# Both MLP products of a decoder layer as seven products of halves, with the activations kept in DRAM between them

## The chip, the cores and the metric

The kernel runs on one core of a Trainium2 chip. The metric is the device time of one execution in microseconds, given as the median of several runs. The engines are named as the profile names them: PE is the matrix engine (TensorE), PEld its weight loads, DVE the vector engine, ACT the scalar engine, POOL GpSimd, and SP the engine whose queue issues most DMAs. ACT issues some DMAs too.

## The reference

One decoder layer on x of 1024 positions by 1024 features, all in float32: three parallel token mixers, merged by gates, then an MLP.

```python
h = rms_norm(x, norm_mix[layer])
proj = h @ w_in[layer]
...
branches = jnp.stack([oa, ob, oc], axis=0)
y = jnp.einsum('nbsm,nmd->bsnd', branches, w_branch[layer])
gate = jax.nn.sigmoid(mg.reshape(B, S, N_BRANCH, D_MODEL).astype(jnp.float32)).astype(y.dtype)
x = x + jnp.sum(gate * y, axis=2) @ w_out[layer]
h = rms_norm(x, norm_mlp[layer])
x = x + jnp.square(jax.nn.relu(h @ w_up[layer])) @ w_down[layer]
```

oa, ob and oc are the outputs of the mixers (differential, sliding-window and block-sparse attention). The change concerns what follows y: the product with w_out (called wo), the normalization, and the two products of the MLP, w_up (wu, 1024 x 4096) and w_down (wd, 4096 x 1024).

## The kernel before

**Products.** Every float32 matrix product is done in three matmuls. `split` (L87) writes a value as a high part, a copy on ACT (L90), and a low part, a subtraction on DVE or POOL (L91), each of a type that PE takes at full rate. `mm3` (L112) then adds high·high, high·low and low·high into one bank of PSUM. A bank holds 128x512 numbers; one matmul here multiplies 128x128 by 128x512. `weight` (L93) loads 128x512 weights from DRAM into a raw tile (`wr`) on SP's queue and splits them into `wh` and `wl`, low part on POOL.

**Order.** The order of PE's instructions is that of the code. The order of the instructions of DVE, ACT, POOL and of SP's queue is chosen by a scheduler when the program is built, from what is ready in its own model. Each engine then executes its list strictly in order. Tiles come from pools; with `bufs=n` a name has n buffers in turn, and an instruction that writes one waits for the last reader of what was there. A pool that is released gives its memory to the pools that are opened after it, with the same kind of wait.

**The end of the program** is `merge_and_mlp` (L1151). The branches are multiplied by their matrices and gated; g tiles (from a DRAM tile `gd`, L1122) hold the gates, and `mh`, `ml` receive the two parts of the merged result for all 1024 positions, with the features on the partitions (eight tiles k of 128).

*The wo stage.* The eight tiles of wo are loaded through two raw buffers (`xn`, L1203) and split, with the low part on DVE and POOL by turns. x is loaded into the eight tiles `x1` (L1208, ACT's queue). For each tile t of 128 positions and each half of 512 features PE does 24 matmuls (8 k by 3), and DVE adds the bank to x1 (L1216). `norm_transpose` (L125) squares x1 on ACT (L130), scales it on DVE (L132), and gives back the transposes (L139), which PE does one tile later; the transposed, normalized tile is split into `mh` and `ml`, which wo no longer needs there.

*Up and down.* `up_block` forms two of the 32 groups of 128 hidden features at a time: 24 matmuls for each group and each half of the positions, then Relu on ACT (L1245), the square on DVE (L1246) and a split into `uh`, `ul`. `down_block` multiplies these two groups by their part of wd for all eight tiles and both halves, 6 matmuls a bank, and DVE adds each bank to x1 (L1262). PE does one up block ahead of the down block that uses the one before. The last down block also sends each tile of x1 to `out`.

In all the MLP has 1536 matmuls of 128x512 for up and 1536 for down, and 16 small transposes between.

## Time and profile before

| | |
|---|---|
| median of 3 runs | 2139.64 us (2138.3 to 2140.58) |
| the profiled execution's own time | 2133.3 us |
| its span, first to last instruction | 2131.5 us |
| mean granted PE clock | 0.990 |
| busy DVE / ACT / POOL | 58% / 41% / 32% of the span |
| wo stage begins, first matmul of up, last of down | about 1322, 1418.65, 2127.26 us |

In the profile's rows a group of instructions is named by line, engine, operation and output<-input with buffer numbers left out. A timeline row gives start and duration; in brackets stands how long the engine had been idle before and what ended the idle time. Matmuls overlap in the pipeline, so their durations add to more than the time that passes: what one costs is the distance from its start to the next start. Busy shares are averages over the whole program; the stage that the change touches is the last third of the span.

### The profile page before, as it was taken

How to read it: one execution, taken by the hardware profiler on the slowest of the kernel's cores; microseconds unless marked ns; L12 is line 12 of the kernel's file. 1: busy time of each engine (PE TensorE's matmuls, PEld its weight loads, DVE VectorE, ACT ScalarE, POOL GpSimd, SP SyncE). 2: the span in 40 equal slices, each digit the busy share in tenths (PEclk: the TensorE clock that was granted, in tenths of full speed). 3: DMA queues.
4: the chain of work that ended last, by engine and by line, in shares of the span. 5: the costliest groups of instructions: out<-in, count | busy, mean ns of one | idle time of the engine just before them, and what ended most of it. 6: DMA issues, size and time to landing. Idle time of an engine off the chain costs nothing.

```text
span 2131.5 us, 29645 instructions
## 1 busy us (share of the span) xinstructions
PE 2025.8 (95%) x10190; PEld 1680.4 (79%) x10190; DVE 1228.5 (58%) x3027; ACT 878.3 (41%) x2358; POOL 676.9 (32%) x965
## 2 busy tenths in 40 slices
PE   6999999988899999999998898999999999999999
PEld 6777777788688878888877776888888888888887
DVE  5757677788757676567777537333334433344334
ACT  5355555566546555455555433122222122211210
POOL 4455345454361121261313065022222122211210
PEclk9999999999999999999999898999999999999999
DMA  6131012011301111221324275211111111111101
GB/s 209 49 100 50 3 53 56 21 42 37 97 26 59 49 58 52 69 65 54 118 90 161 86 255 188 79 48 61 50 46 49 40 55 55 45 45 40 54 7 79
DMA packets 85027, 149.14 MB, mean 70 GB/s; under 512 B 10052, under 2 KB 31044, under 8 KB 84876
## 3 DMA queue, kind: packets, MB, share of 16 engines
q1 hardware_dynamic: 80204, 133.61, 20.0%
q10 hardware_dynamic: 4672, 13.63, 1.8%
q8 instruction: 80, 1.31, 0.3%
q14 instruction: 71, 0.58, 0.1%
HBM read 119.89 MB, written 31.26 MB: 71 GB/s over the span
## 4 chain that ended last, share of the span: by engine, by line
PE 77%; DVE 8%; ACT 5%; DMA 3%; issue 3%; POOL 2%; SPq 0%; DVEq 0%; ACTq 0%; POOLq 0%
PE mm L115 19%; PE mm L116 18%; PE mm L117 18%; PE sc L697 5%; PE tr L745 3%; PE sc L115 2%; PE sc L116 2%; PE sc L117 2%; ACT p L729 2%; PE ac L887 2%; PE ac L888 2%; DMA g<-gd 1%; PE tr L544 1%; DVE sc L721 1%; POOL wl L91 1%
## 5 line engine op out<-in xcount | busy, mean ns | idle before, releaser
L91 POOL TENSOR_TENSOR wl<-wr,wh 128x512 fp32r<-128x512 f32 (+3 forms) x278 | 348.1, 1261 | 698.2 <-ACT wh L90 645.6
L90 ACT ACTIVATE wh<-wr 128x512 fp32r<-128x512 f32 (+3 forms) x290 | 170.8, 596 | 420.7 <-PE mm L117 239.0
L1262 DVE TENSOR_TENSOR x<-x,mm 128x512 f32<-128x512 f32 x256 | 174.7, 687 | 141.0 <-PE mm L117 141.0
L697 PE MATMUL sc<-st 128*128 128x256 f32 (+5 forms) x736 | 200.5, 354 | 16.1 <-ACT p L729 15.8
L1246 DVE TENSOR_TENSOR u<-v 128x512 f32<-128x512 f32 x64 | 64.9, 1014 | 241.0 <-ACT v L1245 241.0
L115 PE MATMUL mm<-mh,wh 128*128 128x512 f32 x512 | 202.0, 395 | 0.2 <-ACT mh L90 0.2
L116 PE MATMUL mm<-ml,wh 128*128 128x512 f32 x512 | 201.9, 394 | 0.2 <-DVE ml L91 0.2
L117 PE MATMUL mm<-mh,wl 128*128 128x512 f32 x512 | 201.8, 394 | 0.0
L116 PE MATMUL mm<-wl,uh 128*128 128x512 f32 x512 | 199.3, 389 | 0.0
L115 PE MATMUL mm<-wh,uh 128*128 128x512 f32 x512 | 199.3, 389 | 0.0
L117 PE MATMUL mm<-wh,ul 128*128 128x512 f32 x512 | 199.2, 389 | 0.0
L90 ACT ACTIVATE ph<-tr 128x384 fp32r<-128x384 f32 (+3 forms) x280 | 138.3, 496 | 117.8 <-PE tr L745 99.9
L91 DVE TENSOR_TENSOR pl<-tr,ph 128x384 fp32r<-128x384 f32 (+3 forms) x280 | 155.5, 558 | 44.4 <-ACT ph L90 40.9
L697 PEld LDWEIGHTS sc<-st 128*128 128x128 f32 x736 | 125.6, 190 | 56.2 <-ACT p L729 24.0
L115 PE MATMUL mm<-hh,wh 128*128 128x512 f32 x384 | 159.5, 415 | 0.0
L117 PE MATMUL mm<-hh,wl 128*128 128x512 f32 x384 | 152.0, 396 | 0.0
L116 PE MATMUL mm<-hl,wh 128*128 128x512 f32 x384 | 151.9, 396 | 0.0
L745 PE MATMUL tr<-ident,p 128*128 128x128 f32 x792 | 132.1, 280 | 15.4 <-ACT o L875 7.9
L742 POOL MEMSET ph<- 128x128 f32 x152 | 34.5, 227 | 298.9 <-PE ac L887 245.5
L729 ACT ACTIVATE p<-sc,mc 128x256 f32<-128x256 f32 (+5 forms) x200 | 106.7, 538 | 50.2 <-DVE mc L721 48.0
L887 PE MATMUL ac<-ph,st 128*128 128x256 f32 x392 | 110.6, 300 | 17.7 <-DVE ob L894 11.3
L115 PE MATMUL mm<-wh,hh 128*128 128x384 f32 (+1 forms) x320 | 125.0, 391 | 0.0
(253 smaller groups left out, 4741.9 us busy)
## 6 DMA issues: line engine op xcount, KB each, us to landing
wr<-wu SPq DMA_DIRECT2D x64, 256.0 KB, 2.6
wr<-wd SPq DMA_DIRECT2D x64, 256.0 KB, 2.9
gd<-go SPq DMA_DIRECT2D x48, 256.0 KB, 2.0
g<-gd SPq DMA_DIRECT2D x48, 256.0 KB, 3.0
wr<-wg SPq DMA_DIRECT2D x40, 256.0 KB, 2.7
wr<-wbr SPq DMA_DIRECT2D x40, 256.0 KB, 3.0
x<-x ACTq DMA_DIRECT2D x16, 512.0 KB, 6.2
wr<-wa SPq DMA_DIRECT2D x32, 192.0 KB, 3.1
```

What stands on the lines that cost most here:

```text
L90: nc.scalar.activation(hi, src, AF.Copy)
L91: (eng or nc.vector).tensor_tensor(lo, src, hi.bitcast(F32), op=ALU.subtract)
L115: mm(out, lh, rh, start=first, stop=False)
L116: mm(out, lh, rl, start=False, stop=False)
L117: mm(out, ll, rh, start=False, stop=last)
L697: self.nc.tensor.matmul(ps[:, off:off + k1 - k0], q[:, t * P:(t + 1) * P], k[:, k0:k1], start=i == 0, stop=i == 1)
L729: self.nc.scalar.activation(p, ps, AF.Exp, bias=m, scale=-1.0, accum_out=l)
L745: nc.tensor.transpose(pt[0:rows, o:o + P], src, self.ident)
L887: nc.tensor.matmul(ac, v, ph, start=first, stop=False)
L888: nc.tensor.matmul(ac, v, pl, start=False, stop=last)
L1246: nc.vector.tensor_tensor(u, v, v, op=ALU.mult)
L1262: nc.vector.tensor_tensor(x1[t][:, cs], x1[t][:, cs], ps, op=ALU.add)
```

## The change

The program after the merge is a new function, `tail`. A matrix product of two matrices cut into 2x2 blocks is formed of seven block products instead of eight, with sums of blocks as operands:

- Of the left matrix the sums s1 = 21 + 22, s2 = s1 − 11, s3 = 11 − 21, s4 = 12 − s2 are formed, of the right one t1 = 12 − 11, t2 = 22 − t1, t3 = 22 − 12, t4 = 21 − t2 (numbers name blocks by row and column). Product i uses the operands of the tables `ASIDE` and `BSIDE`.
- Product 2 accumulates on the bank of 1, 7 on that of 6, and 3 on that of 5.

*Up.* The hidden features are the rows and the positions the columns of the result; the 32 groups are taken as 16 pairs (p, p + 16). A pair has 7 products of 4 k by 3 matmuls: 84 for one pair, 1344 in all. The weight sums s1 to s4 of a pair are formed on DVE and split with the low part on POOL. The sums t1 to t4 of the activations (positions 0 to 511 against 512 to 1023) are made once in the wo stage, by `operands`, for t = 4 to 7, which needs `rb`, copies of the transposes of tile t − 4; so the tiles are taken in the order 0, 4, 1, 5, 2, 6, 3, 7. Two x1 buffers are used, and x1 goes to DRAM (`xd`). In `up_pair` DVE puts the result together out of the banks, ACT does Relu and the square, DVE forms the four sums that down needs as its left operand, and seven tiles of 128x512 go to DRAM (`ud`) for each pair.

*Down.* It begins when up has ended. x1 comes back from `xd` on ACT's queue (8 loads), into memory that up's operands held. Two pairs make a block: for each of the seven products two tiles u come from `ud` and are split on DVE, and two wd operands are split on POOL, which also forms the sums t1 to t4 of wd; 4 banks get 6 matmuls each, 168 in a block, 1344 in all. DVE adds each bank to x1, or, for products 1, 6 and 7, to sums `a1`, `a6`, `a7`. After the last block's products 6 and 7 DVE adds these sums to x1, in 20 more operations.

The core of the diff:

```diff
+    ORDER = (1, 6, 5, 2, 7, 4, 3)
+    ASIDE = {1: "11", 2: "12", 3: "s4", 4: "22", 5: "s1", 6: "s2", 7: "s3"}
+    BSIDE = {1: "11", 2: "21", 3: "22", 4: "t4", 5: "t1", 6: "t2", 7: "t3"}
...
+        xp = tc.alloc_tile_pool(name="xp", side="left", **kw)
...
         for k in range(KT):
-            raw = up.tile([P, D], F32, name="xn", tag="xn", bufs=2)
+            raw = xp.tile([P, D], F32, name="xn", tag="xn", bufs=2)
             nc.sync.dma_start(raw, a["wo"][k])
             self.split(*wo[k], raw, nc.vector if k % 2 else nc.gpsimd)
...
+                if t < 4:
+                    for half in range(2):
+                        r = xp.tile([P, 512], F32, name="rb", tag=f"rb{half}", bufs=1)
+                        self.first[half] = r
+                        nc.scalar.activation(r, ps[half], AF.Copy)
+                        ks = slice(half * 4, half * 4 + 4)
+                        self.split(mh[:, ks, ts], ml[:, ks, ts], wide(r), nc.gpsimd)
+                    return
+                b11, b21 = self.first
+                tmp = lambda: xp.tile([P, 512], F32, name="tt", tag="tt", bufs=3)
+                t1, t2 = tmp(), tmp()
+                nc.vector.tensor_tensor(t1, ps[0], b11, op=ALU.subtract)
+                nc.vector.tensor_tensor(t2, ps[1], t1, op=ALU.subtract)
+                self.split(mh[:, 4:8, ts], ml[:, 4:8, ts], wide(ps[1]))
+                self.split(th["t2"][0][:, :, js], th["t2"][1][:, :, js], wide(t2))
+                self.split(mh[:, 0:4, ts], ml[:, 0:4, ts], wide(t1), nc.gpsimd)
...
+        for t in (0, 4, 1, 5, 2, 6, 3, 7):
...
+            nc.sync.dma_start(xd[t], x1)
...
+            def product(i, chain=None):
+                w = splitted(get(self.ASIDE[i]), nc.gpsimd)
+                bh, bl, k0, s = moving[self.BSIDE[i]]
+                ps = o.ps[i] = o.ps[chain] if chain else self.mm()
+                for k in range(4):
+                    ks = slice(k * P, k * P + P)
+                    self.mm3(ps, w[0][:, ks], w[1][:, ks], bh[:, k0 + k, s], bl[:, k0 + k, s],
+                             k == 0 and not chain, k == 3, bool(chain))
...
+            def act(c):
+                u = temp()
+                nc.scalar.activation(u, c, AF.Relu)
+                nc.scalar.activation(u, u, AF.Square)
+                return u
...
+                for i in self.ORDER:
+                    nc.sync.dma_start(ud[p, i], get(self.ASIDE[i]))
...
+        tf.release()
         mp.release()
+        acc = tc.alloc_tile_pool(name="acc", side="left", **kw)
+        x1 = [acc.tile([P, D], F32, name=f"x1{t}") for t in range(NT)]
+        for t in range(NT):
+            nc.scalar.dma_start(x1[t], xd[t])
...
+        G = 2
+        order = (1, 6, 2, 7, 5, 4, 3)
...
+                for q in range(G):
+                    u = temp()
+                    nc.sync.dma_start(u, ud[b + q, i])
+                    forms.append((splitted(u, nc.vector), splitted(gets[q](self.BSIDE[i]), nc.gpsimd)))
...
+                    if i in sums and b == 0:
+                        nc.scalar.activation(dst, ps, AF.Copy)
+                    else:
+                        nc.vector.tensor_tensor(dst, dst, ps, op=ALU.add)
```

How the change moves instructions is seen in the lists of the two programs. **SP's queue at the end of the third branch, before.** g are the gates of that branch, wr<-wbr its weights, wr<-wu the first weights of up, and xn<-wo the raw tiles of wo:

```order
L1122 DMA g_14891<-gd_86 128x512
L1203 DMA xn_15428<-wo 128x1024
L1203 DMA xn_15432<-wo 128x1024
L1122 DMA g_14914<-gd_86 128x512
L100 DMA wr_15205<-wbr 128x512
L1122 DMA g_14931<-gd_86 128x512
L100 DMA wr_15230<-wbr 128x512
L1203 DMA xn_15436<-wo 128x1024
L1203 DMA xn_15440<-wo 128x1024
L100 DMA wr_15255<-wbr 128x512
```

The same queue with the change, from the load of g_15211, the tenth of the third branch's sixteen:

```order
L1122 DMA g_15211<-gd_86 128x512
L1245 DMA xn_15424<-wo 128x1024
L1245 DMA xn_15428<-wo 128x1024
L1122 DMA g_15236<-gd_86 128x512
L1122 DMA g_15261<-gd_86 128x512
L1245 DMA xn_15432<-wo 128x1024
L1245 DMA xn_15436<-wo 128x1024
L1122 DMA g_15286<-gd_86 128x512
L1122 DMA g_15311<-gd_86 128x512
L1245 DMA xn_15440<-wo 128x1024
L1245 DMA xn_15444<-wo 128x1024
```

Before, the first wo tiles are loaded among the gates of the second branch and the beginning of the third, and the last pair behind g_15286; with the change all eight come behind g_15211, and the last two (not shown) behind four loads of wu. Each pair waits for the low parts of the pair before.

**ACT at the end of up.** u are the last pair's activations, x10 to x17 the tiles of x1 that come back from xd:

```order
L1388 ACTIVATE u_18803<-u_18803 128x512
L1433 DMA x10_18848<-xd_15385 128x1024
L1433 DMA x11_18849<-xd_15385 128x1024
L1387 ACTIVATE u_18825<-u_18720 128x512
L1433 DMA x12_18850<-xd_15385 128x1024
L1433 DMA x13_18851<-xd_15385 128x1024
L1388 ACTIVATE u_18825<-u_18825 128x512
L1433 DMA x14_18852<-xd_15385 128x1024
```

And SP's queue at the same place, from the stores of the last pair's sums to the first loads of down:

```order
L1396 DMA ud_15386<-u_18829 128x512
L1396 DMA ud_15386<-u_18831 128x512
L1396 DMA ud_15386<-u_18836 128x512
L1457 DMA u_18876<-ud_15386 128x512
L1396 DMA ud_15386<-u_18840 128x512
L1457 DMA u_18888<-ud_15386 128x512
L1457 DMA u_18932<-ud_15386 128x512
```

Nothing of the kind stands in the program before, where x1 stays in place and u too. The loads of x1 wait for the last matmul of up, and u_18876 stands behind stores that wait for the last pair's sums; the loads and these stores use DMA semaphores in turn, and u_18876 also waits for the load of x13, u_18888 for that of x15.

**POOL in a block of down.** fl are low parts (of wr or of a sum u), u the sums t1 to t4, wr raw weights of wd:

```order
L91 TENSOR_TENSOR fl_19945<-u_19942,fh_19944 128x512
L91 TENSOR_TENSOR fl_19987<-wr_19706,fh_19986 128x512
L1224 TENSOR_TENSOR u_20114<-wr_20108,u_20112 128x512
L91 TENSOR_TENSOR fl_19997<-wr_19724,fh_19996 128x512
L1224 TENSOR_TENSOR u_20210<-wr_20090,wr_20092 128x512
L91 TENSOR_TENSOR fl_20037<-wr_20034,fh_20036 128x512
```

The load of wr_20108 goes into a buffer that fl_19987 reads last, and the sum that needs it is the next operation of POOL. Before, POOL did only the low parts of the weights in the MLP.

More of the change, by code (lines that the diff above doesn't have):

```diff
@@ L110, in spare, with mm3 @@
         return self.nc.vector if self.alone and k % 2 else self.nc.gpsimd
[L112 removed]
+    def mm3(self, out, lh, ll, rh, rl, first, last, more=False):
         mm = self.nc.tensor.matmul
[L115 to L117 removed]
+        mm(out, lh, rh, start=first, stop=False, skip_group_check=more)
+        mm(out, lh, rl, start=False, stop=False, skip_group_check=more)
+        mm(out, ll, rh, start=False, stop=last, skip_group_check=more)
     def rnorm(self, out, ss, n, width):
@@ L1194, in merge_and_mlp, with sums, get @@
                                                    op0=ALU.mult, op1=ALU.subtract)
+        self.wp.release()
+        self.tail(mp, mh, ml, halves)
+    ORDER = (1, 6, 5, 2, 7, 4, 3)
+    ASIDE = {1: "11", 2: "12", 3: "s4", 4: "22", 5: "s1", 6: "s2", 7: "s3"}
+    BSIDE = {1: "11", 2: "21", 3: "22", 4: "t4", 5: "t1", 6: "t2", 7: "t3"}
+    def sums(self, raw, new, side, eng):
+        made = {}
+        sub, add = ALU.subtract, ALU.add
+        rules = dict(s1=("21", "22", add), s2=("s1", "11", sub), s3=("11", "21", sub), s4=("12", "s2", sub),
+                     t1=("12", "11", sub), t2=("22", "t1", sub), t3=("22", "12", sub), t4=("21", "t2", sub))
+        def get(name):
+            if name not in made:
+                if name in rules:
+                    x, y, op = rules[name]
+                    x, y = get(x), get(y)
+                    made[name] = new()
+                    eng.tensor_tensor(made[name], x, y, op=op)
+                else:
+                    made[name] = raw(name)
+            return made[name]
+        return get
@@ new lines, in tail @@
+    def tail(self, mp, mh, ml, halves):
+        tc, nc, a = self.tc, self.nc, self.a
+        kw = dict(bufs=1, reuse_waits="tile")
+        H = FF // P // 2
+        xd = self.dram.tile([NT, P, D], F32, name="xd")
+        ud = self.dram.tile([H, 8, P, 512], F32, name="ud")
+        pre = tc.alloc_tile_pool(name="pre", side="right", **kw)
+        tf = tc.alloc_tile_pool(name="tf", side="left", **kw)
+        th = {n: [tf.tile([P, 4, 512], F32R, name=f"{n}{x}") for x in range(2)] for n in ("t2", "t3", "t4")}
@@ L1209, in merge_and_mlp @@
+        self.first = [None, None]
         late = []
-        for t in range(NT):
+        for t in (0, 4, 1, 5, 2, 6, 3, 7):
             ts = slice(t * P, t * P + P)
+            x1 = xp.tile([P, D], F32, name="x1", tag="x1", bufs=2)
+            nc.scalar.dma_start(x1, a["x"][ts, :])
             for s in halves:
@@ new lines, in tail, with form, raw @@
+        main = more = None
+        count = dict(f=0, r=0)
+        def form():
+            count["f"] += 1
+            if count["f"] <= 2:
+                return [pre.tile([P, 512], F32R, name=f"f{x}", tag=f"f{x}", bufs=2) for x in "hl"]
+            return [main.tile([P, 512], F32R, name=f"f{x}", tag=f"f{x}", bufs=10) for x in "hl"]
+        def raw(src):
+            count["r"] += 1
+            pool = pre if main is None or count["r"] % 2 else main
+            r = pool.tile([P, 512], F32, name="wr", tag="wr", bufs=4)
+            nc.sync.dma_start(r, src)
+            return r
@@ new lines, in up @@
+        def up(o, todo):
+            for i in todo:
+                o.product(i, {2: 1, 7: 6, 3: 5}.get(i))
+                o.after(i)
+        pairs = [up_pair(0)]
+        pairs[0].product(1)
+        for wp in reversed(wps):
+            wp.release()
+        main = tc.alloc_tile_pool(name="main", side="right", **kw)
+        pairs[0].after(1)
+        pairs.append(up_pair(1))
+        up(pairs[1], (1,))
+        pairs[0].product(2, 1)
+        while late:
+            late.pop()()
+        pairs[1].product(2, 1)
@@ new lines, in tail @@
+        xp.release()
+        more = tc.alloc_tile_pool(name="more", side="right", **kw)
+        for o in pairs:
+            o.after(2)
+        for o in pairs:
+            up(o, [i for i in self.ORDER if i not in (1, 2)])
+        for p in range(2, H):
+            up(up_pair(p), self.ORDER)
+        tf.release()
+        mp.release()
+        acc = tc.alloc_tile_pool(name="acc", side="left", **kw)
+        x1 = [acc.tile([P, D], F32, name=f"x1{t}") for t in range(NT)]
+        for t in range(NT):
+            nc.scalar.dma_start(x1[t], xd[t])
@@ L1280, in layouts @@
+        acc.release()
+        more.release()
+        main.release()
+        pre.release()
 def layouts(inputs):
```

179 lines of the change are left out of this document (115 added, 64 removed).

## The prediction

> **What bounds the kernel now.** I read the page's busy shares first, then its chain of waits, then busy time in windows over the stage that the change rewrites.
>
> ```profile
> PE 2025.8 (95%) x10190; PEld 1680.4 (79%) x10190; DVE 1228.5 (58%) x3027; ACT 878.3 (41%) x2358; POOL 676.9 (32%) x965
> ...
> PE 77%; DVE 8%; ACT 5%; DMA 3%; issue 3%; POOL 2%; SPq 0%; DVEq 0%; ACTq 0%; POOLq 0%
> ```
>
> TensorE is busy 95% of the span and holds 77% of the chain that ended last. An average could hide stages with another limit, so I look at the end of the program by itself. The columns of the windows are the stretch, its length, then busy time (and instructions) of PE, PEld, DVE, ACT and POOL, the granted clock, the DMA share and GB/s.
>
> ```profile
> 1320.00:1360.00 40.00, 35.65 (x147) 28.31 (x146) 20.68 (x27) 9.42 (x16) 4.95 (x4) 0.87 0.43 156
> ...
> 1420.00:1500.00 80.00, 79.52 (x347) 64.21 (x346) 31.37 (x40) 25.57 (x46) 30.25 (x23) 1.00 0.24 77
> 1500.00:1600.00 100.00, 100.00 (x435) 81.30 (x434) 39.29 (x53) 23.13 (x38) 23.39 (x19) 1.00 0.16 48
> ...
> 2000.00:2100.00 100.00, 100.00 (x437) 81.60 (x436) 39.99 (x58) 16.05 (x26) 12.72 (x10) 1.00 0.05 14
> ```
>
> From 1420 us on PE has no idle time at full clock, while DVE is busy 40%, ACT 23% and POOL 23%. The MLP is purely PE-bound: a matmul taken out is worth its full spacing, as long as no other engine becomes the limit. The spacing is read from the first and last matmul of the MLP on the timeline (start, duration, engine, line, operation).
>
> ```profile
> 1418.65 0.48 PE L115 MATMUL mm<-mh,wh 128*128 128x512 f32 x1
> ...
> 2127.26 0.39 PE L117 MATMUL mm<-wh,ul 128*128 128x512 f32 x1
> 2127.69 0.69 DVE L1262 TENSOR_TENSOR x<-x,mm 128x512 f32<-128x512 f32 x1 [0.67 <-PE mm L117]
> ```
>
> Between them the code issues 3072 matmuls of 128x512, so one costs (2127.26 − 1418.65)/3071 = 0.2307 us. The 0.39 us beside each row is its time in the pipeline, not its price. The two halves differ a little; a stretch of up shows 39 spacings in 9.10 us, 0.2333, which leaves 2 × 0.2307 − 0.2333 = 0.228 for down:
>
> ```profile
> 1426.91 0.39 PE L115 MATMUL mm<-mh,wh 128*128 128x512 f32 x1
> ...
> 1436.01 0.40 PE L115 MATMUL mm<-mh,wh 128*128 128x512 f32 x1
> ```
>
> **The sum, part by part.** All of it is made against the profiled execution, 2133.3 us; the median shown, 2139.64 us, lies 6.3 us above it, and I carry the difference to the median.
>
> **Removed.** Seven products for eight leave 2 × 1344 = 2688 matmuls. 384 × 0.2307 = **−88.6 us**.
>
> **wo stage.** The change moves the loads of the eight raw wo tiles behind the tenth of the third branch's sixteen g loads on SP's queue, as four rounds through two buffers. Where these stand now:
>
> ```profile
> 1271.43 0.81 SPq L1203 DMA_DIRECT2D xn<-wo  x2
> ...
> 1307.14 1.64 SPq L1122 DMA_DIRECT2D g<-gd  x2
> ...
> 1315.71 1.06 SPq L1203 DMA_DIRECT2D xn<-wo  x2
> ...
> 1319.65 1.06 ACT L90 ACTIVATE wo<-xn 128x1024 fp32r<-128x1024 f32 x1 [2.68 <-DMA xn<-wo]
> ...
> 1320.79 2.53 POOL L91 TENSOR_TENSOR wo<-xn,wo 128x1024 fp32r<-128x1024 f32 x1 [0.93 <-ACT wo L90]
> ...
> 1326.74 0.79 PE L116 MATMUL mm<-wo,mh 128*128 128x512 f32 x1 [1.72 <-DVE wo L91]
> ```
>
> A round is landing (1315.71 to 1319.65, 3.9) + ACT 1.06 + POOL 2.53 = 7.5 us. That tenth g load is the first of the row at 1307.14, so four rounds end near 1307.5 + 4 × 7.5 = 1337.5, where PE now resumes at 1326.74: **+10 us**. With a landing of 2.9, as the smaller wd loads have (row below), a round is 6.5 and the end 1333.5 (+7); with one of 4.9 it is 8.5, and 1341.5 (+15).
>
> **wo to up.** Today PE goes over without a hole. Now tile 3's transposes stand behind tile 7's matmuls and the first product needs their result at once, and behind Square on ACT:
>
> ```profile
> 1418.49 0.60 ACT L90 ACTIVATE mh<-tr 128x512 fp32r<-128x512 f32 x1 [9.76 <-PE tr L139]
> 1418.99 1.05 ACT L130 ACTIVATE xn<-x 128x1024 f32<-128x1024 f32 x1
> 1419.94 0.19 ACT L130 ACTIVATION_READ_ACCUMULATOR xn<-x 128x1 f32 x1
> ...
> L91 POOL TENSOR_TENSOR wl<-wr,wh x121: 1279/1285/1747, 1428.7 to 2065.1; 128x512 fp32r<-128x512 f32 x121
> ```
>
> Copy 0.60, Square 1.05 + 0.19, copy 0.60, mh 0.60, ml on POOL 1.285: 4.3, so PE idles about 4 us. Four products of two pairs then run. Product 6 needs t2 of tile 7, three DVE operations and a split behind up to eight weight sums on DVE, of 0.69 each (row of ul below): 2.1 + 0.6 + 0.7 − 2.8 (the product in front, 12 × 0.2333) + 0 to 5.5 = 0.6 to 6.1; I take 3.6. Product 5 needs t1's low part, on POOL behind nine forms, 9 × 1.285 = 11.6, of which 2.8 at least is covered: 0 to 8.8, I take 5. Such holes also cost clock:
>
> ```profile
> 1328.18 0.63 PE L116 MATMUL mm<-wo,mh 128*128 128x512 f32 x1
> 1328.61 0.63 PE L117 MATMUL mm<-wo,ml 128*128 128x512 f32 x1
> ...
> 1332.45 0.54 PE L117 MATMUL mm<-wo,ml 128*128 128x512 f32 x1
> 1332.83 0.39 PE L115 MATMUL mm<-wo,mh 128*128 128x512 f32 x1
> 1333.06 0.40 PE L116 MATMUL mm<-wo,mh 128*128 128x512 f32 x1
> ```
>
> After the wait at 1326.74 matmuls go every 0.425 us until 1332.45 and then every 0.23: 13 × 0.197 = 2.6 us lost (the window of 0.87 clock). Sum 4 + 3.6 + 5 + 2.6 = **+15**, bounds 4 + 0.6 = 5 and 4 + 6.1 + 8.8 + 2.6 = 22.
>
> By the Trainium skill, "TensorE: Matmul & The Clock Gate", Part 1, the array falls to half rate after about 3.4 us of idle and needs about 3.4 us of work to come back, in a free-running window; by that the cold stretch after a hole costs half of 3.4, an estimate of 1.7 us, and the sum would be about 2 us lower (two holes). The 2.6 us of the rows is larger, and followed a wait of only 1.72 us; the measurement decides.
>
> **up, steady.** A pair is 84 matmuls, 84 × 0.2333 = 19.6 us. Beside it stand on DVE 5 operations that read PSUM and 8 with two SBUF operands, 13 × 0.69 = 9.0; on ACT 16 × 0.60 = 9.6; on POOL 7 × 1.285 = 9.0. When DVE and POOL both read two SBUF operands they stop each other:
>
> ```profile
> 1427.13 13.33 POOL L91 TENSOR_TENSOR wl<-wr,wh 128x512 fp32r<-128x512 f32 x9 [6.12 <-ACT wh L90]
> ...
> 1428.18 1.01 DVE L91 TENSOR_TENSOR ul<-u,uh 128x512 fp32r<-128x512 f32 x1 [0.70 <-ACT uh L90]
> 1433.35 1.30 DVE L1246 TENSOR_TENSOR u<-v 128x512 f32<-128x512 f32 x1 [4.16 <-ACT v L1245]
> 1436.00 1.60 DVE L91 TENSOR_TENSOR ul<-u,uh 128x512 fp32r<-128x512 f32 x1 [1.36 <-ACT uh L90]
> ...
> L91 DVE TENSOR_TENSOR ul<-u,uh x63: 691/693/1599, 1436.0 to 2086.2; 128x512 fp32r<-128x512 f32 x63
> L1262 DVE TENSOR_TENSOR x<-x,mm x256: 674/689/690, 1467.9 to 2127.7; 128x512 f32<-128x512 f32 x128
> ```
>
> Nine POOL operations took 13.33 instead of 9 × 1.285 = 11.57: 0.59 more for each of the three DVE operations inside, which themselves took 0.3 to 0.9 more than 0.69. DVE adds that read PSUM (last row) never did in 256. With 8 × 0.6 on both sides DVE comes to 14, POOL to 14: below 19.6, so **0** (to +8 over 16 pairs if half a microsecond shows through).
>
> **up to down.** The x1 tiles come back from DRAM, eight loads of 512 KB on ACT's queue, into memory that the last up matmul still reads; the first ud loads share semaphores with these loads and stand on SP behind the last pair's stores. Nothing of it can begin before the last up matmul.
>
> ```profile
> x<-x ACTq DMA_DIRECT2D x16, 512.0 KB, 6.2
> ...
> wr<-wd SPq DMA_DIRECT2D x64, 256.0 KB, 2.9
> ```
>
> x1 landing 6.2 + waits on the lane 2 + ud landing 2.9 + copy 0.60 + split 0.69 + 1 issuing = 13.4, and 2.6 of clock: **+16**. Without the sharing it is the last pair's chain: DVE 0.69 + two ACT 1.2 + four sums 2.8 + 2.9 + 1.3 = 9. With a second landing behind the first it is 16 + 5 = 21.
>
> **down, steady.** A block of two pairs is 168 matmuls, 168 × 0.228 = 38.3 us. POOL does 14 splits of weights and 8 sums, 22 × 1.285 = 28.3, and stops for 14 u splits of DVE, 14 × 0.69 = 9.7: 38.0. DVE does 28 adds × 0.69 = 19.3 and 14 × (0.69 + half a POOL operation, 0.64) = 18.6: 37.9. Both stand at the bound with no slack, and each block has a place where a wd load waits for a POOL split to free its buffer, and the POOL sum right behind waits for that load (landing 2.9, some covered). I take 38.0 + 1.8 = 39.8 for a block, 1.5 over PE's 38.3: **+12** over 8 blocks; 0 if it is covered, +20 with the whole landing less 0.4.
>
> **Tail.** The last block has 20 more adds on DVE, 13.8 us, and the last matmuls go onto banks which these adds keep back: 37.9 + 13.8 = 51.7 against 38.3, of which the adds between early products lie beside matmuls. **+8**, bounds 3 and 14. The 4 us from the last add to the end stay.
>
> Sum: −88.6 + 10 + 15 + 0 + 16 + 12 + 8 = −27.6. On the profiled execution 2105.7, on the median **2112.0 us**. Lower bounds: −88.6 + 7 + 5 + 0 + 9 + 0 + 3 = −64.6, 2075. Upper: −88.6 + 15 + 22 + 8 + 21 + 20 + 14 = +11.4, 2151.
>
> **Rivals.**
> 1. *PE stays the bound in both new stages and the holes are short.* For it: DVE 40% and POOL 23% today leave room, and the tables put POOL and DVE just under 38.3. Against it: no slack for any wait. Down 0 and holes at their lower ends are the lower sum, **2075**.
> 2. *DVE bounds down, slower than before.* If each of DVE's 14 splits waits for a whole POOL operation (1.285) rather than half, a block is 19.3 + 14 × (0.69 + 1.285) = 47.0, and down costs 8 × 8.7 = 70 rather than 12: −27.6 + 58 = +30, **2170**. It decides from (27.6 + 12)/8 = 5 us a block, 43.3 us. For it: the 1.60 row, 0.91 over. Against it: the mean over the three rows is 0.61, and POOL is not always running.
> 3. *The handover through DRAM is longer.* If the x1 loads delay the first ud loads and wd loads in a chain (6.2 + 6.2 + 2.9 + 2.9 more for a second product), it costs 30: **2126**, still faster.
> 4. *The products fewer, but not the time.* Three of seven products accumulate on another's bank, which ACT or DVE must first have read: 48 such places in up at 0.6 us are +29, **2141**, no change. Against it: one to two other products (2.8 to 5.6 us) stand between in the order.
>
> The Trainium skill, "SBUF — State Buffer", section "Who interferes with whom", states that such a VectorE and GpSimd pair exclude each other for whole instructions and issue order decides who blocks. By that rule every split that arrives behind an operation waits for its rest and, if POOL's next one gets in first, for a whole one more, which is rival 2 and its 2170. The rows at 1427 agree with the exclusion; which order down gets, no row of before shows.
>
> **How the numbers follow.** Chances: forecast 0.65 (2085 to 2135), rival 1 0.12, rival 2 0.10, rival 3 0.09, rival 4 0.04. The range leaves out rival 2 and half of rival 1: **2074 to 2146**. A measurement of this kernel can tell about 0.2% (4.3 us) from no change. Faster: 0.62 of the forecast + 0.12 + 0.09 = 0.83; same: rival 4 and 0.02 of the forecast's upper end, 0.06; slower: rival 2 and 0.01 of that end, 0.11.
>
> **What would show it.** Up pairs at 19.6 us and 0.2333 a matmul; one PE hole of about 14 us between the last Square and the first down matmul, ended by a u split; PE near 96% in down windows with POOL above 90% busy; first wo stall on a wo split near 1337; clock below 1 after each hole. The forecast is wrong if down windows show PE below 85%, if up shows PE waiting for DVE sums, or if the holes add to less than 20 us.

## The result and the profile after

The changed kernel takes **2100.26 us** (median of 4 runs, 2098.98 to 2102.18); the kernel before, beside it, 2139.5 us. The ratio is 0.9817 with a 95% interval of 0.98 to 0.9834, that is 39 us less. The forecast was 2112 us, with a range of 2074 to 2146. The profiled execution took 2099.69 us, with a span of 2097.7 us. Single runs that fell into a slower state of the chip (3891.08 us in one experiment) are left out.

The page of the changed kernel, busy time by engine:

```profile
PE 1949.8 (93%) x9806; PEld 1614.9 (77%) x9806; DVE 1387.6 (66%) x3207; ACT 1018.7 (49%) x2614; POOL 957.4 (46%) x1141
```

PE lost 76 us of work and 2 points of its share: the program got shorter and got holes. Where they are is shown by the windows (stretch, length, busy time of PE, PEld, DVE, ACT, POOL, granted clock, DMA share, GB/s):

```profile
1420.00:1440.00 20.00, 15.81 (x60) 12.47 (x60) 14.61 (x14) 8.92 (x17) 13.48 (x9) 0.83 0.30 100
...
1500.00:1600.00 100.00, 100.00 (x431) 80.55 (x430) 49.68 (x67) 49.52 (x83) 48.66 (x36) 1.00 0.43 145
...
1760.00:1780.00 20.00, 1.00 (x2) 0.49 (x3) 7.71 (x7) 5.01 (x9) 9.08 (x7) 0.59 0.99 369
...
1800.00:1900.00 100.00, 100.00 (x443) 82.81 (x442) 79.40 (x107) 41.55 (x76) 86.77 (x59) 1.00 0.48 150
...
2050.00:2098.00 48.00, 38.79 (x163) 30.99 (x161) 43.94 (x59) 9.96 (x19) 19.74 (x13) 0.96 0.34 115
```

PE is the bound in the middle of up (1500 to 1600) and of down (1800 to 1900), at full clock; the losses stand at the start of up, in one hole at 1760, and at the end. The timeline of PE has each of them (start, duration; in brackets the idle time before it, and what ended it):

```profile
1337.48 0.79 PE L116 MATMUL mm<-wo,mh 128*128 128x512 f32 x1 [1.69 <-POOL wo L91]
...
1431.23 0.50 PE L115 MATMUL mm<-mh,fh 128*128 128x512 f32 x1 [2.35 <-ACT mh L90]
1433.57 0.80 PE L116 MATMUL mm<-ml,fh 128*128 128x512 f32 x1 [1.84 <-POOL ml L91]
...
1448.54 0.50 PE L115 MATMUL mm<-t,fh 128*128 128x512 f32 x1 [0.23 <-ACT t L90]
1452.29 0.50 PE L116 MATMUL mm<-t,fh 128*128 128x512 f32 x1 [3.25 <-DVE t L91]
...
1461.47 0.47 PE L115 MATMUL mm<-t,fh 128*128 128x512 f32 x1 [2.00 <-DVE u L1368]
...
1476.92 0.50 PE L115 MATMUL mm<-t,fh 128*128 128x512 f32 x1 [1.22 <-DVE u L1368]
...
1759.58 0.40 PE L117 MATMUL mm<-mh,fl 128*128 128x512 f32 x1
...
1777.38 0.80 PE L115 MATMUL mm<-fh 128*128 128x512 f32 x1 [17.40 <-ACT fh L90]
...
2081.49 0.79 PE L117 MATMUL mm<-fh,fl 128*128 128x512 f32 x1 [3.03 <-DVE fl L91]
...
2092.55 0.39 PE L117 MATMUL mm<-fh,fl 128*128 128x512 f32 x1
```

Runs of one and the same kernel differ by several us here (those of the kernel before in the later comparisons lay from 2131 to 2143). The first 1220 us, which no experiment changes, end between 1219.7 and 1228.0 in the profiles. The experiments are therefore judged by the lengths of stages, from the starts of first and last matmuls in their profiled executions. A stage that an experiment leaves alone repeats within about 1 us (down 315.2 to 316.3, the gap in front of it 17.2 to 17.8, up 328.35 to 328.44):

| kernel | wo resumes at | last wo to first up | up, first to last matmul | to first of down | down, first to last |
|---|---|---|---|---|---|
| changed | 1337.48 | 3.62 | 328.35 | 17.80 | 315.17 |
| e1_wo_early | 1336.13 | 3.62 | 333.40 | 17.78 | 316.00 |
| e2_tr_mid | 1335.86 | 0.23 | 332.09 | 17.32 | 315.96 |
| e9_three_pairs | 1335.14 | 0.24 | 330.67 | 17.67 | 316.25 |
| e10_dve_first | 1332.62 | 0.24 | 326.76 | 17.60 | 316.34 |
| e3_x1_late | 1339.03 | 3.62 | 328.38 | 8.75 | 316.60 |
| e4_prefetch | 1338.15 | 3.62 | 338.35 | 0.23 | 324.93 |
| e11_s_loads | 1335.56 | 3.62 | 328.39 | 0.23 | 320.92 |
| e5_no_adds | 1339.16 | 3.62 | 328.36 | 17.83 | 309.61 |
| e12_all | 1335.37 | 0.24 | 327.50 | 0.23 | 321.35 |

At full speed up would take 1343 × 0.2333 = 313.3 us. Down would take 1343 × 0.228 = 306.2 at the pace that the forecast used; the changed kernel's own pace there is 0.2267 (mean of the spacings from 1900 to 2000 us), which gives 304.5.

### The profile page after: what moved, and what is told of

Read it like the earlier page. It is cut to its first block, busy times and chain, and to the rows that moved or that the text cites. A ratio compares the mean times of both kernels' runs of the same rounds, so it can differ in the third digit from the quotient of the medians.

```text
span 2097.7 us, 30506 instructions
## 1 busy us (share of the span) xinstructions
PE 1949.8 (93%) x9806; PEld 1614.9 (77%) x9806; DVE 1387.6 (66%) x3207; ACT 1018.7 (49%) x2614; POOL 957.4 (46%) x1141
## 3 DMA queue, kind: packets, MB, share of 16 engines
q10 hardware_dynamic: 5824, 17.83, 2.5%
## 5 line engine op out<-in xcount | busy, mean ns | idle before, releaser
L91 POOL TENSOR_TENSOR wl<-wr,wh 128x512 fp32r<-128x512 f32 (+4 forms) x150 | 180.9, 1213 | 209.8 <-ACT wh L90 159.6
L90 ACT ACTIVATE fh<-u 128x512 fp32r<-128x512 f32 x176 | 100.4, 622 | 179.6 <-PE mm L116 97.7
L91 POOL TENSOR_TENSOR fl<-wr,fh 128x512 fp32r<-128x512 f32 x96 | 146.0, 1525 | 86.3 <-ACT fh L90 86.3
L115 PE MATMUL mm<-fh 128*128 128x512 f32 x352 | 138.5, 393 | 17.4 <-ACT fh L90 17.4
L91 DVE TENSOR_TENSOR fl<-u,fh 128x512 fp32r<-128x512 f32 x112 | 121.5, 1089 | 40.7 <-ACT fh L90 31.3
L117 PE MATMUL mm<-fh,fl 128*128 128x512 f32 x352 | 138.6, 394 | 4.2 <-DVE fl L91 4.2
L116 PE MATMUL mm<-fl,fh 128*128 128x512 f32 x352 | 138.5, 393 | 1.7 <-POOL fl L91 1.6
L91 POOL TENSOR_TENSOR fl<-s,fh 128x512 fp32r<-128x512 f32 x64 | 86.3, 1352 | 79.9 <-ACT fh L90 79.9
L90 ACT ACTIVATE wh<-wr 128x512 fp32r<-128x512 f32 (+4 forms) x162 | 90.5, 568 | 63.1 <-PE mm L116 33.8
L888 PE MATMUL ac<-pl,st 128*128 128x256 f32 x392 | 106.8, 293 | 5.8 <-DVE pl L91 5.0
```

The source lines that it names most:

```text
L90: nc.scalar.activation(hi, src, AF.Copy)
L91: (eng or nc.vector).tensor_tensor(lo, src, hi.bitcast(F32), op=ALU.subtract)
L115: mm(out, lh, rh, start=first, stop=False, skip_group_check=more)
L116: mm(out, lh, rl, start=False, stop=False, skip_group_check=more)
L117: mm(out, ll, rh, start=False, stop=last, skip_group_check=more)
L888: nc.tensor.matmul(ac, v, pl, start=False, stop=last)
```

## The experiments

### The wo stage: is it the rounds through two buffers?

```diff
+        rw = tc.alloc_tile_pool(name="rw", side="left", **kw)
         xp = tc.alloc_tile_pool(name="xp", side="left", **kw)
...
-            raw = xp.tile([P, D], F32, name="xn", tag="xn", bufs=2)
+            raw = rw.tile([P, D], F32, name="xn", tag=("xn", "x1")[k // 2 % 2], bufs=2)
```

> The changed kernel with one difference: the eight raw tiles of wo go through four buffers in a pool of their own, whose memory is free during the third branch, instead of through two in a pool that waits for the second branch's memory; four loads can go early and two rounds are left of four. Theory (the start of the wo stage is late by rounds of load, copy and subtraction): PE resumes the first wo group without holes near 1327 to 1330 us instead of 1337.5, and the time falls by 7 to 10 us from 2100.3, to 2090 to 2093. Rival (the end of the third branch itself sets it, through gates that now come late): the first group ends as before and the time falls by at most 2 us.

Measured: 2098.23 us (2092.55 to 2104.65: two runs near 2093 and two near 2104, and the profile is of the longest). wo resumes at 1336.13, only 1.4 us earlier than in the changed kernel, but in this profile the branches begin 2.4 us later. The times are therefore better counted from the branches (the first matmul of the second branch's product and the last of the third's, from the timelines):

| kernel | first branch matmul | last branch matmul | last to wo resuming | first to wo resuming | first to last wo matmul |
|---|---|---|---|---|---|
| before | 1220.12 | 1315.71 | 11.03 | 106.62 | 197.50 |
| changed | 1224.48 | 1312.08 | 25.40 | 113.00 | 203.13 |
| e1_wo_early | 1226.88 | 1317.36 | 18.77 | 109.25 | 200.25 |

In the other eleven kernels with the change, whose wo loads are those of the changed kernel, the third of these columns holds 23.6 to 26.3 us and the fourth 111.2 to 115.1. So with two rounds in place of four PE resumes 6.6 us sooner after the branches, close to the 7 to 10 of the theory. That the rounds hold the loads back is also seen in what SP's queue of the changed kernel waits for from 1295 to 1332 (us in all, times, longest):

```profile
SPq L1245 <- POOL wo L91: 7.0, 3, 3.5
SPq L1245 <- DVE wo L91: 4.5, 3, 2.0
```

Little of it reaches the end. The branches themselves take 90.48 us instead of 87.60, with a new wait for a gate, and up takes 5.0 us more, where PE waits 5.52 us for tile 7's operands. That the four early loads delay the gate's load would explain the first; no run tests it, nor why tile 7's operands come later. PE and SP in the timeline of e1:

```profile
1253.14 0.50 PE L115 MATMUL mm<-ob,wh 128*128 128x512 f32 x1 [1.46 <-DVE g L1178]
```

```profile
1299.54 18.21 SPq L1122 DMA_DIRECT2D g<-gd  x6
1317.84 1.65 SPq L1246 DMA_DIRECT2D xn<-wo  x2
...
1320.18 2.64 SPq L1246 DMA_DIRECT2D xn<-wo  x2
```

The last four loads stand behind six g loads, which took from 1299.54 to 1317.75 to get out, and their copies on ACT come in one row at 1327.06, behind the branch's own. So the rounds are a part of the delay, and the place of the last loads and copies in queues that the third branch still fills is another. That a load on another queue would shorten it was not tried.

### From wo to up: where do the holes go?

Transposes between the halves of a tile:

```diff
                 nc.vector.tensor_tensor(x1[:, s], x1[:, s], ps, op=ALU.add)
+                while late:
+                    late.pop()()
             nc.sync.dma_start(xd[t], x1)
-            while late:
-                late.pop()()
```

> The changed kernel with one difference: in the wo stage the transposes of the tile before stand between the two halves of a tile's matmuls instead of behind them, so tile 3's operands are formed while PE works on tile 7. Theory (PE idles because tile 3's operands are only begun when the last wo matmul is done): the holes of 2.35 and 1.84 us in front of the first up product and about 2.5 us of cold clock go, and the time falls by 5 to 7 us, to 2093 to 2095; the holes of 3.25 and 2.00 us behind tile 7 stay. Rival (tile 7's chain on DVE and POOL sets the end, and time won before it is waited there): the later holes grow by as much, and the time falls by at most 1.5 us.

Measured: 2102.53 us (2101.44 to 2107.61). The hole in front of up goes (3.62 to 0.23), and up gets longer by 3.7 us: the rival is right, and what was gained is waited for at tile 7's operands and behind (2.91, 2.06 and 5.10 us there instead of 0.23, 3.25 and 2.00). Up doesn't begin earlier after wo resumes either, 94.25 us against 93.75: tile 3's transposes now lie within the wo stage, and PE waits three times 0.5 us for a scaled tile. DVE and POOL of the changed kernel in that stretch show what tile 7's operands stand behind:

```profile
1435.67 1.77 DVE L1224 TENSOR_TENSOR s<-wr 128x512 f32<-128x512 f32 x1
1437.36 1.78 DVE L1224 TENSOR_TENSOR s<-wr,s 128x512 f32<-128x512 f32 x1
...
1451.09 1.15 DVE L91 TENSOR_TENSOR t<-tt,t 128x512 fp32r<-128x512 f32 x1
```

```profile
1433.46 3.43 POOL L91 TENSOR_TENSOR fl<-wr,fh 128x512 fp32r<-128x512 f32 x2
1436.84 1.75 POOL L91 TENSOR_TENSOR ml<-rb,mh 128x512 fp32r<-128x512 f32 x1
1438.54 5.15 POOL L91 TENSOR_TENSOR fl<-s,fh 128x512 fp32r<-128x512 f32 x3
```

A sum on DVE starts every 1.70 us and an operation on POOL every 1.70 us: where both have two SBUF operands and always more to do, they take turns one by one, and a sum that takes DVE 0.69 us alone takes 1.77. Tile 7's t2 comes out of that queue at 1452. Two experiments on top of this kernel. The first gives PE 5.6 us of work that needs none of it, from a third pair:

```diff
-        pairs.append(up_pair(1))
-        up(pairs[1], (1,))
+        for p in (1, 2):
+            pairs.append(up_pair(p))
+            up(pairs[p], (1,))
...
         pairs[1].product(2, 1)
+        pairs[2].product(2, 1)
```

> The kernel with transposes between the halves of a tile, and with one further difference: products 1 and 2, which need no operand of the last tile, are done for three pairs instead of two before product 6 of the first pair (and a third buffer for the copy of product 1). Theory (in the first 30 us of up DVE's sums and POOL's low parts take turns, 1.70 us for one of each, and PE waits for tile 7's operands in that queue; 5.6 us more of matmuls that need none of it cover the wait): the holes of the first 40 us of up fall from 11 us to at most 4, up takes 324 to 327 us instead of 332.1, and the time falls by 5 to 8 us against the kernel with transposes between the halves. Rival (the third pair's low parts stand in the same queue on POOL and delay tile 7's as much): up stays above 330 us.

Measured: 2102.39 us (2100.51 to 2105.08); up 330.67 against 332.09. The rival is right: more cover brings more low parts into POOL's queue, and the wait for t2 is then 5.8 us. The second takes POOL out of it:

```diff
-                w = splitted(get(self.ASIDE[i]), nc.gpsimd)
+                w = splitted(get(self.ASIDE[i]), nc.vector if p < 2 else nc.gpsimd)
```

> The kernel with transposes between the halves of a tile, and with one further difference: the low parts of the weights of the first two pairs of up are formed on DVE instead of POOL, so the two engines hardly take turns there. Theory (at the start of up DVE and POOL do one operation each in 1.70 us because both read two SBUF operands, and that rate keeps tile 7's operands and the first sums from PE): alone, DVE does one in 0.69 us, twenty-two sums and low parts take 15 us, and the holes of the first 40 us of up fall from 11 us to under 5; up takes 317 to 323 us instead of 332.1. Rival (the chain from tile 7's last matmul over its square, scaling, transposes and sums sets the holes, whoever forms the low parts): up stays above 328 us.

Measured: 2098.29 us (2094.11 to 2102.43); up 326.76, between the two. DVE of this kernel:

```profile
1431.88 0.69 DVE L1224 TENSOR_TENSOR s<-s,wr 128x512 f32<-128x512 f32 x1
1432.49 0.68 DVE L1224 TENSOR_TENSOR s<-wr 128x512 f32<-128x512 f32 x1
...
1446.70 0.68 DVE L91 TENSOR_TENSOR t<-tt,t 128x512 fp32r<-128x512 f32 x1
```

Alone, DVE starts a sum every 0.60 us. Without the turns up is 332.09 − 326.76 = 5.3 us shorter. The rest of the hole stays (PE waits 2.85 and 5.21 us for tile 7's operands), since DVE's fixed order has t2's low part at 1446.70 behind sums and low parts that are needed later. That an order with tile 7 first would close it was not tried.

### From up to down: the x1 loads or the last pair?

```diff
-        for t in range(NT):
-            nc.scalar.dma_start(x1[t], xd[t])
...
                         nc.scalar.activation(dst, ps, AF.Copy)
+                        if i != 7:
+                            t = j if i == 1 else 4 + j
+                            nc.scalar.activation(x1[t][:, 0:1], ps[:, 0:1], AF.Copy)
+                            nc.scalar.dma_start(x1[t], xd[t])
```

> The changed kernel with one difference: each load of x1 from DRAM at the start of down waits for a bank of down's first or second product (by an operation on ACT of one column that writes x1 ahead of the load), so the 4 MB no longer stand in front of the first loads of the activations. Theory (the 17.4 us hole is the x1 loads' 11 us at full DMA rate with the first activations behind them): the hole shrinks to what the last pair's chain needs, 8 to 10 us, and the time falls by 7 to 9 us, to 2091 to 2093. Rival (the last pair's sums and stores on SP's queue set the hole, or the loads come back as a wait at product 2): the time falls by less than 3 us.

Measured: 2093.8 us (2092.88 to 2094.08); the gap falls from 17.80 to 8.75, as the theory had it, and down grows by 1.4 us only. SP of the changed kernel, with the loads of x1 ahead, and then of this one:

```profile
1757.19 10.33 SPq L1396 DMA_DIRECT2D ud<-u  x5
1768.42 0.32 SPq L1457 DMA_DIRECT2D u<-ud  x1
1770.34 0.32 SPq L1396 DMA_DIRECT2D ud<-u  x1
1772.17 6.79 SPq L1457 DMA_DIRECT2D u<-ud  x7
```

```profile
1754.77 11.44 SPq L1396 DMA_DIRECT2D ud<-u  x5
1766.30 0.40 SPq L1455 DMA_DIRECT2D u<-ud  x1
1767.56 0.92 SPq L1396 DMA_DIRECT2D ud<-u  x2
1768.53 6.75 SPq L1455 DMA_DIRECT2D u<-ud  x8
```

The last up matmul stands at 1759.58 and 1761.46. So the first u load goes out 8.8 us after it in the changed kernel and 4.8 us with late x1 loads, and the second 12.6 and 7.1 us. Half of the hole was the x1 loads. Two things tie the others to them, and no run separates the two: the window at 1760 shows 369 GB/s and a DMA share of 0.99, and SP's queue waited 9.5 us for x1 tiles to land from 1755 to 1785 (5.0 with loads and 4.5 with stores next in it). The other half stands behind the last pair's stores. To take the second half away, I first formed product 1's operands ahead of the last pair's end:

```diff
+        o = up_pair(H - 1)
+        up(o, self.ORDER[:-2])
+        gets0 = blocks(0)
+        forms0 = operands(0, gets0, 1)
+        up(o, self.ORDER[-2:])
```

> The kernel with late x1 loads, and with one further difference: the operands of down's first product of the first block (two activation tiles, two weight tiles) are loaded and split ahead of the last pair's last two products, so they don't stand behind the last pair's stores. Theory (of the 8.4 us that were left between up and down, all is the last pair's chain on SP's queue): the first down matmul follows the last up matmul within 1 us, product 1 covers 5.5 us, and 2 to 4 us of waiting come at product 6; against the kernel with late loads 4 to 6 us less, near 2088 to 2090. Rival (the operands of product 6 wait as long as before): the hole moves to product 6 whole, and the time stays within 2 us of 2093.8.

Measured: 2104.09 us (2102.21 to 2107.73), a miss on both sides. On ACT the copies for down (from 1757.77) stand ahead of those that up's own last two products need, and product 6's loads still come among the last stores and behind them (from 1776.82). Its PE shows two holes in place of one:

```profile
1760.52 0.79 PE L115 MATMUL mm<-t,fh 128*128 128x512 f32 x1 [5.43 <-ACT fh L90]
...
1786.02 0.80 PE L115 MATMUL mm<-fh 128*128 128x512 f32 x1 [9.88 <-ACT fh L90]
```

What may keep the loads back is buffers: u tiles come from one ring of 12, which the last pair holds. With another ring for the first four, which down doesn't otherwise use:

```diff
-                    u = temp()
+                    u = temp("s" if b == 0 and i in (1, 6) else "u")
```

> The kernel with late x1 loads, and with one further difference: the four activation tiles of down's first two products go into buffers of another ring (one that down doesn't use), so their loads don't wait for buffers of the last pair and stand ahead of its last stores. Theory (the 8.75 us left between up and down come from these tiles' buffers and their place behind the last stores, and from nothing that down's first products compute): the gap falls under 1.5 us and at most 2 us come back at product 2; the time falls by 7 to 9 us against the kernel with late loads, to 2085 to 2087. Rival (as with the operands formed early, the hole moves to a later product whole): gap and new holes together stay above 7 us.

Measured: 2091.28 us (2086.74 to 2092.65). Down begins 0.23 us after up, so the loads' buffers and their place were the rest of the gap (which of the two isn't separated). Its PE:

```profile
1766.16 0.50 PE L115 MATMUL mm<-fh 128*128 128x512 f32 x1 [1.78 <-ACT fh L90]
1767.50 0.80 PE L116 MATMUL mm<-fl,fh 128*128 128x512 f32 x1 [0.84 <-POOL fl L91]
1769.84 0.80 PE L115 MATMUL mm<-fh 128*128 128x512 f32 x1 [1.12 <-ACT fh L90]
1772.85 0.79 PE L116 MATMUL mm<-fl,fh 128*128 128x512 f32 x1 [2.21 <-POOL fl L91]
```

Gap and down together are 321.15 us, against 325.35 with late x1 loads alone and 332.97 in the changed kernel: 4.2 of the 8.5 us of gap are kept, and 4.3 come back. The four holes, 5.95 us together, all stand at the first bank of product 6, whose operands come next, and not at product 2 as the theory had it. Between the forecast's two cases, nearer to the rival's.

### Down: how near is POOL to being the bound?

Two kernels add operations on POOL to each block, used by nothing; the first four, the second seven:

```diff
+                for _ in range(1 if i in (1, 6, 7, 4) else 0):
+                    nc.gpsimd.tensor_tensor(spare, spare, spare, op=ALU.add)
```

> The changed kernel with four more operations on POOL in each block of down (a tile of zeros added to itself, 128x512, used by nothing). Theory (POOL was mis-priced but is the nearest bound of down: 33.4 us busy and 2.7 us of waiting for a load in a block of 38.3, so 2.2 us are free): four operations of 1.29 to 1.71 overrun that by 2.9 to 4.6 us a block, and down takes 338 to 352 us instead of 315. Rival (down has room, since POOL's low parts and sums run far ahead of PE): down stays under 323 us.

> The changed kernel with seven more operations on POOL in each block of down instead of four. Four more made down 320.6 us, 5.4 over the changed kernel, so POOL still had room for nearly all of them. Theory (29 operations of 1.285 and 14 stops of 0.47 for DVE make 43.9 us at most, 37.3 without a stop, against PE's 38.3): down becomes bound by POOL, 1 to 5 us a block, and takes 328 to 360 us. Rival (DVE's splits are spread so thinly that POOL is hardly stopped): under 325 us.

Measured: down 320.57 us with four, the rival's side, and 332.27 with seven, within the theory's range (2105.39 and 2117.93 us, one run each). As a price for each block they tell little, since nothing tied the additions to a block: all 32 of the first kernel ran between 1737 and 1828 us, at the end of up, in the gap and in the first block and a little more. But they fill POOL in stretches, and these give its capacity. Windows of about one block, with seven:

```profile
1838.00:1876.00 38.00, 34.85 (x145) 27.87 (x144) 29.62 (x37) 13.09 (x24) 38.00 (x29) 0.96 0.44 141
1876.00:1914.00 38.00, 36.46 (x160) 29.52 (x159) 31.19 (x41) 15.38 (x28) 38.00 (x28) 1.00 0.43 135
...
1952.00:1990.00 38.00, 38.00 (x167) 31.00 (x166) 33.55 (x42) 14.91 (x28) 35.19 (x25) 1.00 0.44 146
```

and the changed kernel:

```profile
1838.00:1876.00 38.00, 38.00 (x169) 31.48 (x168) 30.94 (x43) 15.37 (x28) 32.78 (x23) 1.00 0.48 153
```

With 28 or 29 operations POOL is full and PE loses 1.5 to 3 us; with 25 POOL has 2.8 us left and PE loses none; the kernel has 22 to 23 and 32.8 us. POOL comes to be the bound at more than 25 and at most 28 operations a block.

The last one tests what makes POOL's operations longer than alone. It leaves out the low parts of the activations in down:

```diff
-                    forms.append((splitted(u, nc.vector), splitted(gets
+                    f = form()
+                    nc.scalar.activation(f[0], u, AF.Copy)
+                    nc.vector.tensor_scalar(f[1], u, 0.0, None, op0=ALU.mult)
+                    forms.append((f, splitted(gets
```

> The changed kernel with the low parts of the activations left out in down: DVE writes zeros there by an operation that reads one SBUF operand (the tile times 0) in place of the subtraction of two. Theory (only DVE operations with two SBUF operands take turns with POOL): POOL's low parts and sums fall to 1.28 to 1.30 us each in down from a mean of 1.5, DVE's operation is not stretched, and the time stays within 3 us, since PE is the bound either way. Rival (any DVE operation that reads SBUF takes turns with POOL): POOL's mean stays at 1.5.

Measured: 2102.77 us (one run), down 312.41. The groups of the stretch 1800 to 2050 (count | busy, mean ns of one | idle before) in the changed kernel and in this one:

```profile
L91 DVE TENSOR_TENSOR fl<-u,fh 128x512 fp32r<-128x512 f32 x92 | 94.9, 1032 | 24.6 <-ACT fh L90 18.0 <-POOL fl L91 3.0 <-POOL u L1224 2.4
L91 POOL TENSOR_TENSOR fl<-u,fh 128x512 fp32r<-128x512 f32 x53 | 79.9, 1517 | 3.7 <-ACT fh L90 3.1 <-DMA u<-ud 0.6
```

```profile
L1460 DVE TENSOR_SCALAR fl<-u 128x512 fp32r<-128x512 f32 x91 | 82.2, 904 | 3.3 <-POOL fl L91 3.1 <-DVE a L1475 0.2
L91 POOL TENSOR_TENSOR fl<-u,fh 128x512 fp32r<-128x512 f32 x53 | 70.5, 1340 | 16.7 <-ACT fh L90 16.7
...
L1460 DVE TENSOR_SCALAR fl<-u x91: 412/844/1535, 1804.2 to 2049.0; 128x512 fp32r<-128x512 f32 x91
```

POOL's mean falls from 1.52 to 1.34 us, but not to 1.285, and DVE's operation, 0.41 us at its shortest, takes 0.84 in the median: this operation with one SBUF operand takes turns too, only it holds POOL for less. Neither side as it was put.

### The tail, and all together

```diff
-                    if i == 6:
+                    if i == 6 and False:
...
-                    elif i == 7:
+                    elif i == 7 and False:
```

> The changed kernel without the 20 additions on DVE in the last block that bring products 1, 6 and 7 of all blocks into x1; that part of the result is left out, to price the tail. Theory (these additions delay a split of DVE that product 4 waits for, 3.0 us and the cold clock behind it, and about 1 us at the very end): the time falls by 5 to 6 us, to 2094 to 2095. Rival (the last block is bound by DVE all along): the time falls by 10 us or more.

Measured: 2096.07 us (2092.03 to 2099.30); down 309.61 against 315.17, so the 20 additions cost 5.6 us before the last matmul, and from there to the end of the span 4.0 us remain (2093.9 − 2089.86) where the changed kernel has 5.15: 6.7 us in all, a little more than the 5 to 6 of the theory, and far from the rival's 10.

> The changed kernel with the differences together: transposes between the halves, the first two pairs' low parts on DVE, late x1 loads, the first activation tiles in the other ring, and in the last block the products in the order 1, 6, 7, 2, 5, 4, 3, so that the 20 additions have four products beside them instead of three. If the holes add up independently: 2100 less 3 (wo to up), less 9 to 14 (start of up), less 16 (up to down), less 2 to 4 (tail), 2063 to 2071 us, and faster than both kernels. Rival (what is gained at one place is waited for at the next): above 2080 us.

Measured: 2086.72 us (median of 6 runs, 2085.74 to 2103.15), a ratio of 0.9765 (0.9741 to 0.9789) to the kernel before, whose interval doesn't meet the changed kernel's. It is faster than both kernels, but the rival is right on the sum. Of what each edit had won, the table keeps 4.6 us of up against the kernel with transposes between the halves, and what the other ring kept of the handover; the gap behind wo is gone as well, but up begins 94.8 us after wo resumes, no sooner than in the changed kernel (93.75); the new order of the last block brings nothing (down 321.35 with it, 320.92 without), because product 5 now waits 2.37 us for a bank that DVE has yet to read. The kernel with late x1 loads and the other ring alone stands at 0.9768 (0.9754 to 0.9782); the two can't be told apart.

## Why the prediction was right, and which terms were not

**Removed, −88.6 us: right.** In the windows from 1500 and from 1800 PE is busy 100% at full clock, matmuls go every 0.2333 us in up as before and every 0.2267 in down, and 384 fewer are issued.

**wo stage, +10: measured 5.6, under the lower bound of 7.** That PE resumes at 1337.48, where 1337.5 was forecast, is luck, and so is the last wo matmul 10.0 us later than before: 4.4 us of these had passed before the branches began (1224.48 against 1220.12). From there to the last wo matmul it is 203.13 us against 197.50. The rounds are real: behind the last branch matmul PE now resumes after 25.4 us instead of 11.0, and two rounds fewer take 6.6 off (e1). But the first round began 5 us earlier than the sum had it (1302.5 instead of 1307.5), four rounds took 35 us and not 30, and one thing was put at nothing: the branches got 8.0 us shorter (87.60 instead of 95.59). Before, PE waited five times in them for gates, 5.0 us in all; now it never does. The likely cause, which was not tested by itself, is that the first wo loads no longer stand among the loads of those gates; with four of them early again (e1) one such wait is back.

**wo to up, +15: measured 16.** The gap grew from 1.03 to 3.62, and up stands 15.0 over its full speed, of which 1.0 are transposes and 0.5 were there before: 2.6 + 13.5 = 16.1. The first hole (2.35 + 1.84 for 4) and the second (0.23 + 3.25 for 3.6) came in the size forecast. The second did so in part by luck: the eight sums in front of t2 were priced at 0.69 each at most and take 1.70, but they begin at 1432.82, long before tile 7's transposes at 1444.47, and what t2's low part (1451.09) then stands behind is other work of DVE. The third and a fourth, 2.00 and 1.22 (5 forecast), wait for DVE to read product 6's bank and not for t1's low part on POOL. This is the mechanism of rival 4, at two places of its 48. The clock was lost twice, at about 1434 and 1453 (2.7 and 1.6 us), not once, as the sum had it (2.6).

**up, steady, 0: right.** PE 100%, DVE 50%, POOL 49%. The forecast had 14 of 19.6 us for DVE and for POOL, too much for the same reason as in down.

**up to down, +16: measured 21**, at the upper bound: 17.6 us of gap, and 3.4 in which down gets going (309.61 − 306.2 without the tail; 5.1 at the pace of 0.2267). The two causes named, x1 loads and last stores, are both there, 9.05 and 8.52 us (e3, e11). Of rival 3's chain, 30 us, the first part came about: the first loads of down do wait for landings of x1.

**down, steady, +12: measured 0.** This term failed by most. It was 38.0 us of POOL a block and 1.8 us of waiting. POOL is busy 32.8. The stop of a POOL operation for a DVE split was put at the whole 0.69 us for each of 14, while the stretched operations of the trace take 1.75 for 1.285, 0.47, and only part of them are stretched: 23 operations × 1.285 = 29.6, and 3.2 us of stops instead of 9.7. The wait for the wd load is there, and one of its 2.7 us rows a block fits into what is left. The rows of before had shown 0.59 a stop; the sum took 0.69.

**Tail, +8: measured 6.7.**

Together −88.6 + 5.6 + 16.1 + 0 + 21 + 0 + 6.7 = −39.2, which is the difference of the medians (39.2). The two spans differ by 33.8 only, because the profiled execution of before was an early one: 4.4 us of the rest are the head start above. The forecast of −27.6 was 11.6 too high: down 12, wo 4.4 and the tail 1.3 too dear, the handover 5 and the start of up 1 too cheap. That it came within 12 us is in part because these errors cancel; the range was 72 us wide.

Of the signs named in advance, PE is at 100% in the windows of down, better than the 96% named, and POOL at 86% and not above 90; the hole between up and down is 17.4 us, ended by the copy of a u tile on ACT and not by the split behind it. One sign of being wrong did come, at the start of up only: PE waits there for DVE's sums (L1368) and for t2's low part.

Rival 2, down bound by DVE at 47.0 us a block, did not come about. Its price of a split, 0.69 + 1.285 = 1.98, is near what an operation of DVE does take at the start of up (1.77 in the rows at 1435), where both queues are full; in down the splits are spread between adds that read PSUM, and the median is 1.17.

## What to carry to other kernels

When matmuls are taken out of a stage that PE bounds, the steady part pays in full here, and the answer lies in the seams: where the loops used to overlap, each new pass through DRAM or through freed memory was a hole, with matmuls at half speed behind it. Price two engines that stop each other from the stretched rows themselves, and ask whether both queues are full there: full, they fall to one of each in 1.70 us; with gaps, as in down, a DVE split cost POOL 0.23 us in the mean (3.2 for 14), a third of its 0.69. Count a stage's length from a point ahead of everything that the change moves, or the spread of what comes before is taken for the change. Time won at the front of a seam is kept only if the engine that feeds the next operand isn't already behind.

## What the runs showed of the hardware that was not expected

A tensor_scalar on DVE that reads a single SBUF operand of 128x512 in float32 (0.41 us at its shortest) also takes turns with POOL. POOL in the timeline of the kernel without low parts of activations:

```profile
1848.81 1.30 POOL L91 TENSOR_TENSOR fl<-u,fh 128x512 fp32r<-128x512 f32 x1 [0.66 <-ACT fh L90]
1850.06 1.49 POOL L91 TENSOR_TENSOR fl<-wr,fh 128x512 fp32r<-128x512 f32 x1
```

Stretched operations take 1.47 to 1.49 us there instead of 1.29, and those beside a two-operand subtraction (0.69 alone) 1.75. So POOL is held for about 0.2 us less than DVE's operation takes. The Trainium skill, "SBUF — State Buffer", section "Who interferes with whom", says that tensor_scalar can contend when it enters a two-port mode, and that the engine that comes second is blocked for the whole instruction. That it contends, the runs agree; in which mode it ran, they don't show; and the delay is less than the whole instruction, 0.47 of 0.69 and 0.19 of 0.41.

After the holes of 2.35 and 1.84 us at 1431 the clock came back only at 1439.3, after 5.7 us of matmuls every 0.43 us, and the hole of 3.25 us was followed by matmuls at nearly full speed before the spacing went to 0.43 us (until 1456.51):

```profile
1452.63 0.39 PE L117 MATMUL mm<-t,fl 128*128 128x512 f32 x1
...
1453.12 0.63 PE L116 MATMUL mm<-t,fh 128*128 128x512 f32 x1
1453.55 0.63 PE L117 MATMUL mm<-t,fl 128*128 128x512 f32 x1
```

In these rows the stretch at half speed thus begins and ends some microseconds after the hole, and part of a hole's price is paid where PE has work.
